# A four-layer hybrid decoder on one core: the layer-1 gate stored as twice its silu, the final gain moved to the last multiply, 1/rms per 512 tokens, and an earlier first norm

## The chip, the cores and the metric

The kernel runs on one core of a Trainium2 chip. The metric is the device time of one execution in microseconds; each comparison takes the median of several executions. TensorE (PE) does the matmuls, VectorE (DVE), ScalarE (ACT) and GpSimd (POOL) the elementwise work, and SyncE (SP), ACT and POOL issue DMAs. Each engine takes its instructions in the order in which they stand in its stream: one that waits holds back all behind it.

## The reference

The batch is 1, with 2048 tokens of width 1024 in fp32. The "layers" of the code are 0 and 1 (DEPTH = 2):

```
for i in range(2):
    hn = rmsnorm(h, norm_gain[i])
    if i == 0:   h = h + even_mixer(hn)      # retention and stick-breaking attention, gated
    else:        h = h + rwkv7_mixer(hn)     # r, k, v, g projections and a recurrence over tokens
    gate = sigmoid(h @ ple_gate[i])
    h = h + gate * (p[i] @ ple_proj[i])
return rmsnorm(h, final_gain)

# the part of rwkv7_mixer that the change touches
    y = head_norm(y, LNX_EPS) * lnx_g + lnx_b
    y = y + bonus
    out = (y * silu(g)) @ w_out
```

## The kernel before

**Tiling.** A token half `w` is 1024 tokens, a block `TB` is 512 tokens, a feature block is 128 rows (`NB` = 8 of them). The fp32 product is made of three matmul passes over a high and a low part of both operands (L239, L240, L241); `split` (L199 and L200) makes the parts: ACT casts the high part, and DVE or POOL subtracts it to get the low part. Raw weights pass through the buffer `wraw`, of which there is one; the split weights `w` are also written to DRAM as `parts` and read from there when they are used again.

**Order of the work.** Retention of half 0 (0 to 300 us), stick-breaking attention (to 500), `tail` of layer 0 (to 715: output projection, per-layer input, sum of squares `ssacc`), `l1_proj(0)` (to 1175: norm, the r, k, v, g projections and what the recurrence needs); retention and attention of half 1 (to 1690); `recur(0)`, the recurrence of half 0, merged with `tail_lean` for layer 0 of half 1 (to 2381, the first matmuls of `l1_proj(1)` beside its end); `l1_proj(1)` (to 2855); `recur(1)` merged with `tail_lean` for layer 1, three blocks of 512 tokens (to 3555); `tail` of layer 1 for the last block with `finish`, the final norm (to 3710). A scheduler that simulates the engines decides the order of the instructions on each engine when the program is built, so that a changed operation can reorder what stands around it.

**Places that the change touches.**

- At the start, `retention` loads x transposed for both blocks (`l0_in`, L352), then x by rows (`xt`, L367). ACT squares the rows and sums them (L369), DVE makes 1/rms (L335 to L342, L372), PE spreads it over the partitions (`rbp`, L375). The constants `k` (L144) and the `rope` table (L421) are loaded through SP.
- `l1_proj` adds `ssacc` up over the partitions by eight small matmuls (`ssp`, L991), makes 1/rms for 1024 tokens in one chain of DVE operations (L335 to L342), spreads it (`rbp`, L1046) and scales the activations into `hn` (L1064). In between, DVE splits weights for the other matmuls of that stage.
- `g_proj`, the last projection of `l1_proj`, copies each 128x512 result from PSUM to `ev` on ACT (L1108) and ACT issues its store.
- `post` in `recur` finishes a chunk of 64 tokens: POOL scales `y` and makes `vt` times the bonus `bon` (L1603), POOL multiplies `y` by the gain `lnx` (L1604), DVE adds the bias (L1605) and then adds `vt` to `y` (L1607). `gram` in `recur` is PE's L1396 with its evacuations on DVE (L1417, L1421) and ACT (L1420).
- `gated` in `tail_lean` makes m g sigmoid(g): DVE L866, ACT L867, DVE L868. `tail` uses silu on ACT (L713) and DVE L714.
- The final gain is applied in `tail_lean` by DVE (L949) and in `tail` by ACT (L779); `finish` and `tail` then multiply by the spread 1/rms (L830, L797).

## Time and profile before

| | before |
|---|---|
| median of 3 runs | 3716.74 us (3715.48 to 3717.23) |
| profiled execution | 3711.4 us |
| its span | 3709.6 us |
| granted clock, mean | 0.939 |
| PE busy | 3383.3 us, 91% |
| DVE busy | 1991.4 us, 54% |
| ACT busy | 1375.3 us, 37% |
| POOL busy | 971.0 us, 26% |
| DMA, mean | 181 GB/s |

The span is what the profile shows of the execution's own time. Busy shares are averages over stages with different limits; the rows further down are taken from single stages. In the timelines a bracket behind a row gives how long its engine sat idle before it, and what ended that.

### The profile page before, as it was taken

Reading aid. Unit: us, or ns where it says so; the run is one execution under the profiler, and the core shown is the slowest. Engines: PE = TensorE matmul, PEld = TensorE weight load, DVE = VectorE, ACT = ScalarE, POOL = GpSimd, SP = SyncE. Lnnn points to the kernel's source line nnn. Section 1 sums busy time; section 2 is a strip of 40 time slices with the busy share of each in tenths; the row PEclk is TensorE's granted clock in tenths of the full one; section 3 lists DMA queues with packets and bytes.
Section 4 is the critical chain, followed back from the end, with each engine's and each line's share of the span. In section 5 each row is a group of like instructions: output and inputs, shape, how many; then the busy total and the mean of one; then the engine's idle time right before and its main releaser. Section 6 shows DMA issues by size and latency. Waiting matters only on the chain.

```text
span 3709.6 us, 65403 instructions
## 1 busy us (share of the span) xinstructions
PE 3383.3 (91%) x25640; PEld 2694.0 (73%) x25640; DVE 1991.4 (54%) x3959; ACT 1375.3 (37%) x2671; POOL 971.0 (26%) x1019
## 2 busy tenths in 40 slices
PE   7999999899999999999879998699988698978968
PEld 6888878787666788888767776587656577767756
DVE  3435552452665333567856666641574477566543
ACT  4333442354564222445523333343453143223222
POOL 3345554300000222556512222200000243222322
PEclk9999999899999999999989998699999788979979
DMA  7259765655688216537367655333676777656485
GB/s 263 96 171 271 218 195 177 216 164 182 201 266 288 99 67 194 175 101 148 68 203 210 194 177 144 104 121 138 200 249 178 186 222 211 186 144 183 158 281 197
DMA packets 570788, 671.94 MB, mean 181 GB/s; under 512 B 215408, under 2 KB 416368, under 8 KB 539504
## 3 DMA queue, kind: packets, MB, share of 16 engines
q1 hardware_dynamic: 495072, 578.41, 50.2%
q0 software_dynamic: 40576, 33.56, 4.4%
q10 hardware_dynamic: 34832, 55.78, 4.1%
q8 instruction: 203, 3.33, 0.4%
q14 instruction: 105, 0.86, 0.1%
HBM read 419.50 MB, written 248.12 MB: 180 GB/s over the span
## 4 chain that ended last, share of the span: by engine, by line
PE 71%; DMA 10%; DVE 9%; ACT 3%; SPq 3%; issue 3%; POOL 1%; DVEq 0%; ACTq 0%; POOLq 0%
PE pj L239 17%; PE pj L240 17%; PE pj L241 17%; PE g L1396 2%; PE tp L654 1%; DMA nb<-nad 1%; DVE wb L1450 1%; DVE prd L1444 1%; PE lora L1266 1%; SPq L1429 1%; PE u L1516 1%; PE x L1538 1%; DMA xr<-ar 1%; PE z L625 1%; PE ot L240 1%
## 5 line engine op out<-in xcount | busy, mean ns | idle before, releaser
L239 PE MATMUL pj<-act,w 128*128 128x512 f32 x1216 | 498.5, 414 | 27.0 <-ACT act L199 10.5
L241 PE MATMUL pj<-act,w 128*128 128x512 f32 x1216 | 497.9, 410 | 6.0 <-POOL w L200 5.9
L240 PE MATMUL pj<-act,w 128*128 128x512 f32 x1216 | 496.9, 409 | 2.5 <-DVE act L200 1.7
L239 PE MATMUL pj<-xs,w 128*128 128x512 f32 x768 | 296.8, 401 | 21.0 <-ACT xs L199 9.5
L240 PE MATMUL pj<-xs,w 128*128 128x512 f32 x768 | 305.7, 399 | 6.3 <-DVE xs L200 6.2
L241 PE MATMUL pj<-xs,w 128*128 128x512 f32 x768 | 301.5, 395 | 0.0
L239 PEld LDWEIGHTS pj<-act,w 128*128 128x128 f32 x1216 | 238.3, 197 | 83.7 <-ACT act L199 13.1
L241 PEld LDWEIGHTS pj<-act,w 128*128 128x128 f32 x1216 | 238.4, 196 | 60.4 <-POOL w L200 9.0
L240 PEld LDWEIGHTS pj<-act,w 128*128 128x128 f32 x1216 | 238.9, 196 | 54.3 <-DVE act L200 3.0
L239 PE MATMUL pj<-w,act 128*128 128x512 f32 x640 | 257.7, 407 | 19.3 <-ACT w L199 9.8
L240 PE MATMUL pj<-w,act 128*128 128x512 f32 x640 | 256.7, 401 | 2.9 <-POOL w L200 2.9
L241 PE MATMUL pj<-w,act 128*128 128x512 f32 x640 | 254.3, 401 | 0.0
L636 DVE TENSOR_TENSOR_SCAN rr<-om,rr,ones 128x512 f32<-128x512 f32 (+3 forms) x160 | 202.0, 1274 | 46.8 <-ACT om L630 39.2
L645 POOL TENSOR_TENSOR be<-be,rr 128x512 f32<-128x512 f32 (+3 forms) x160 | 176.7, 1107 | 164.4 <-DVE rr L636 82.3
L200 POOL TENSOR_TENSOR w<-wraw,w 128x1024 fp32r<-128x1024 f32 x72 | 162.1, 2253 | 204.1 <-ACT w L199 198.1
L239 PEld LDWEIGHTS pj<-xs,w 128*128 128x128 f32 x768 | 145.4, 190 | 70.3 <-issue 14.5
L240 PEld LDWEIGHTS pj<-xs,w 128*128 128x128 f32 x768 | 145.9, 190 | 43.9 <-DVE xs L200 13.0
L241 PEld LDWEIGHTS pj<-xs,w 128*128 128x128 f32 x768 | 145.9, 190 | 33.9 <-issue 2.7
L1396 PE MATMUL g<-xr,kb 64*128 64x128 f32 x1024 | 116.8, 311 | 52.0 <-DVE grb L1421 23.0
L199 ACT CAST w<-wraw 128x1024 fp32r<-128x1024 f32 x105 | 104.6, 1000 | 144.7 <-DMA wraw<-in_even_w_in 38.7
L239 PEld LDWEIGHTS pj<-w,act 128*128 128x128 f32 x640 | 122.3, 192 | 48.4 <-ACT sg L448 12.1
L458 POOL TENSOR_SCALAR tst<-gs 128x128 f32<-128x128 f32 x64 | 34.4, 538 | 468.8 <-DMA gs<-gstate 246.5
(330 smaller groups left out, 7511.5 us busy)
## 6 DMA issues: line engine op xcount, KB each, us to landing
w<-parts SPq DMA_DIRECT2D x145, 1024.0 KB, 6.0
parts<-w SPq DMA_DIRECT2D x97, 1024.0 KB, 5.5
wraw<-in_odd_w_in SPq DMA_DIRECT2D x32, 512.0 KB, 7.2
ar<-ar SPq DMA_DIRECT2D x32, 512.0 KB, 4.4
w<-v SPq DMA_DIRECT2D x128, 128.0 KB, 3.8
xr<-ar SPq DMA_DIRECT2D x64, 256.0 KB, 5.5
kb<-kb SPq DMA_DIRECT2D x32, 512.0 KB, 5.1
kg<-dk POOLq DMA_DIRECT2D x24, 512.0 KB, 5.0
```

The costliest lines, as they stand in the source:

```text
L199: nc.scalar.copy(hi, src)
L200: (lo_eng or nc.vector).tensor_tensor(lo, src, hi.bitcast(F32), op=ALU.subtract)
L239: nc.tensor.matmul(ps, a[0], b[0], start=first, stop=False)
L240: nc.tensor.matmul(ps, a[0], b[1], start=False, stop=False)
L241: nc.tensor.matmul(ps, a[1], b[0], start=False, stop=last)
L625: nc.tensor.matmul(z[:, :kw], q[:, 1, qc], kt[:, 0, :kw], start=False, stop=True)
L636: nc.vector.tensor_tensor_scan(rr[:, 0:kw][:, ::-1], om[:, ::-1], self.ones.to_broadcast([P, kw]), rr[:, kw : kw + 1], op0=ALU.mult, op1=A ...
L645: nc.gpsimd.tensor_tensor(be, be, rr[:, 1 : kw + 1], op=ALU.mult)
L654: nc.tensor.transpose(tp[:, j], wt[qi][:, j * P : (j + 1) * P], self.ident)
L1266: nc.tensor.matmul(pss[j], w2[jw][hs, oc], mid[jm][hs, sl], start=n == 0, stop=n == 2)
L1396: nc.tensor.matmul(ps[:, j], kb[br, ob], xr[br, par, ob], start=True, stop=True)
L1429: nc.sync.dma_start(nad[b].rearrange("u r t -> r u t"), na[b * 16 : (b + 1) * 16, :, o : o + 16])
```

## The change

- Gates: ACT takes tanh(g/2) from PSUM and DVE computes (tanh + 1) g, which is 2 silu(g); that is stored. The bias of the head norm, halved, stands in the tile `hlb` and is added where the gate is applied: one DVE operation (m + hlb) g takes the place of L866, L867 and L868, and of L713 and L714 in layer 1. So that the sum stays right, `lnx` and `bon` are halved once per recurrence by two new ACT operations, the bias addition L1605 and its loads go.
- Final gain: L949 and L779 go; the last multiply becomes one DVE operation with the gain and the spread 1/rms.
- First norm: loads and squares of block 0 stand ahead of x of block 1; `k` goes to POOL's queue and `rope` to ACT's; for the first head of half 0 the low part of the weights is made by DVE instead of POOL.
- `l1_proj`: 1/rms is made for 512 tokens at a time by `rms(t)`, called at the first feature block of each token block.

```diff
-        nc.sync.dma_start(k, ins["c_mat"][:, 0:C_SCAN])
+        nc.gpsimd.dma_start(k, ins["c_mat"][:, 0:C_SCAN])
...
+                        self.lo_eng = nc.vector if w == 0 else nc.gpsimd
...
-                nc.sync.dma_start(rope, self.i["c_rope"][w * HT : (w + 1) * HT, :].rearrange("(t p) c -> p t c", p=P))
-                self.l0_in(w, sx, 1, range(0, NB))
-                self.l0_stats(w, sx, pq)
+                nc.scalar.dma_start(rope, self.i["c_rope"][w * HT : (w + 1) * HT, :].rearrange("(t p) c -> p t c", p=P))
+                self.lo_eng = nc.gpsimd
                 for tb in range(NTB):
+                    if tb:
+                        self.l0_in(w, sx, tb, range(0, NB))
+                    self.l0_stats(w, sx, pq, [tb])
...
-                        nc.scalar.activation(g, g, AF.Silu)
-                        nc.vector.tensor_tensor(m, m, g, op=ALU.mult)
+                        if l == 0:
+                            nc.scalar.activation(g, g, AF.Silu)
+                            nc.vector.tensor_tensor(m, m, g, op=ALU.mult)
+                        else:
+                            nc.vector.scalar_tensor_tensor(
+                                m, m, self.hlb[:, d : d + 1], g, op0=ALU.add, op1=ALU.mult
+                            )
...
-                    o = sb.tile([P, TB], F32, tag="o", name=self.u("o"))
+                    o = h1[ob] if l else sb.tile([P, TB], F32, tag="o", name=self.u("o"))
...
-                    else:
-                        nc.scalar.activation(h1[ob], o, AF.Copy, scale=self.col(V_GF, ob))
...
-                    nc.vector.tensor_tensor(o, rbp, h1[ob][:, tok(t)], op=ALU.mult)
+                    nc.vector.scalar_tensor_tensor(
+                        o, h1[ob][:, tok(t)], self.col(V_GF, ob), rbp, op0=ALU.mult, op1=ALU.mult
+                    )
...
-                nc.vector.tensor_tensor(m, m, g, op=ALU.mult)
-                nc.scalar.activation(g, g, AF.Sigmoid)
-                nc.vector.tensor_tensor(m, m, g, op=ALU.mult)
+                if l == 0:
+                    nc.vector.tensor_tensor(m, m, g, op=ALU.mult)
+                    nc.scalar.activation(g, g, AF.Sigmoid)
+                    nc.vector.tensor_tensor(m, m, g, op=ALU.mult)
+                else:
+                    nc.vector.scalar_tensor_tensor(m, m, self.hlb[:, d : d + 1], g, op0=ALU.add, op1=ALU.mult)
...
-                if l == 1:
-                    nc.vector.tensor_scalar_mul(o, o, self.col(V_GF, ob))
...
-            rs = self.token_rstd(ev, psn, "rnp")
-            rb = [ev.tile([P, TB], F32, tag="L" if t else "sg", name=self.u("rb")) for t in range(NTB)]
-            for t in range(NTB):
-                rbp = pj[0].tile([P, TB], F32, tag="proj", name=self.u("rbp"))
+            rb, hn = [], []
+
+            def rms(t):
+                rs = self.token_rstd(ev, psn, "rnp", range(4 * t, 4 * t + 4))
+                rb.append(ev.tile([P, TB], F32, tag="L" if t else "sg", name=self.u("rb")))
+                rbp = psn.tile([P, TB], F32, tag="rnp", name=self.u("rbp"))
...
             def normed(d, t):
+                if d == 0:
+                    rms(t)
...
+            def twice_silu(dst):
+                def evac(t, ps):
+                    e = ev.tile([P, TB], F32, tag="ev", name=self.u("ev"), bufs=2)
+                    nc.scalar.activation(e, ps, AF.Tanh, scale=0.5)
+                    nc.vector.scalar_tensor_tensor(e, e, 1.0, ps, op0=ALU.add, op1=ALU.mult)
+                    nc.scalar.dma_start(dst[:, t * TB : (t + 1) * TB], e)
+
+                return evac
+
             def g_proj():
-                yield from self.proj_pairs(load(3), mix(3), lambda ob: to_dram(d_g[ob]), pj)
+                yield from self.proj_pairs(load(3), mix(3), lambda ob: twice_silu(d_g[ob]), pj)
...
-            nc.gpsimd.tensor_tensor(y, y, lnx[0][0], op=ALU.mult)
-            nc.vector.tensor_tensor(vt, vt, lnx[1][0], op=ALU.add)
+            nc.gpsimd.tensor_tensor(y, y, lnx, op=ALU.mult)
...
             for par in range(2):
-                for t, src in lnx:
-                    nc.sync.dma_start(t[half(par)], src[par].unsqueeze(0).to_broadcast([C, NB, C]))
+                nc.sync.dma_start(lnx[half(par)], gain[par].unsqueeze(0).to_broadcast([C, NB, C]))
                 nc.sync.dma_start(bonus[half(par)], self.d_b[par].rearrange("(c t) o -> t c o", t=C))
+            nc.scalar.activation(lnx, lnx, AF.Copy, scale=0.5)
+            nc.scalar.activation(bonus, bonus, AF.Copy, scale=0.5)
```

Three places of the streams follow. The first is SP's, from its first `xt` load to its fourth, at the start of the program (`x` is x transposed, 256 KB; `wraw` a pair of 256 KB weight loads; `parts` a 1 MB store of split weights; `xt` 512 KB). Before:

```order
L367 DMA xt_230<-in_x 128x1024
L352 DMA x_212<-in_xT 128x512
L367 DMA xt_234<-in_x 128x1024
L221 DMA parts_161<-w_155 128x2048
L214 DMA wraw_188<-in_even_w_in 128x4x128 x2
L352 DMA x_216<-in_xT 128x512
L352 DMA x_220<-in_xT 128x512
L352 DMA x_224<-in_xT 128x512
L367 DMA xt_238<-in_x 128x1024
L221 DMA parts_177<-w_171 128x2048
L214 DMA wraw_685<-in_even_w_in 128x4x128 x2
L367 DMA xt_242<-in_x 128x1024
```

In the changed kernel the same place, from the second `parts` store on (all 16 loads of x transposed stand ahead of the fourth `xt` in both):

```order
L223 DMA parts_163<-w_157 128x2048
L216 DMA wraw_190<-in_even_w_in 128x4x128 x2
L354 DMA x_258<-in_xT 128x512
L354 DMA x_262<-in_xT 128x512
L354 DMA x_266<-in_xT 128x512
L354 DMA x_270<-in_xT 128x512
L370 DMA xt_208<-in_x 128x1024
L370 DMA xt_212<-in_x 128x1024
L223 DMA parts_179<-w_173 128x2048
L216 DMA wraw_688<-in_even_w_in 128x4x128 x2
```

The fourth `xt` now stands ahead of the third `parts` store and of the fifth pair of `wraw` loads; before, both stood ahead of it.

The second place is DVE's stream at the start of `l1_proj(0)`, from the last addition to `ssacc` (token block 1) to the last step of the first 1/rms. Before, with 1/rms for 1024 tokens:

```order
L775 TENSOR_TENSOR ssacc<-ssacc,g_6256 128x512
...
L1063 COPY hn_6455<-hnlast 128x1
L335 TENSOR_SCALAR rs_1238_6350<-ssp_6341 128x8
L336 TENSOR_SCALAR rs_1240_6352<-ssp_6341 128x8
L200 TENSOR_TENSOR w_6595<-wraw_6596,w_6595 128x1024
...
L200 TENSOR_TENSOR w_6635<-wraw_6636,w_6635 128x1024
...
L342 SCALAR_TENSOR_TENSOR rs_1239_6351<-rs_1238_6350,rs_1239_6351 128x8
L1064 SCALAR_TENSOR_TENSOR hn_6381<-hx_6382,vec,rb_6366 128x512
```

In the changed kernel, with 1/rms for the first 512 tokens:

```order
L786 TENSOR_TENSOR ssacc<-ssacc,g_6259 128x512
...
L1077 COPY hn_6447<-hnlast 128x1
L337 TENSOR_SCALAR rs_1240_6350<-ssp_6345 128x4
L338 TENSOR_SCALAR rs_1242_6352<-ssp_6345 128x4
L339 TENSOR_SCALAR rs_1241_6351<-rs_1240_6350 128x4
L202 TENSOR_TENSOR w_6615<-wraw_6616,w_6615 128x1024
...
L202 TENSOR_TENSOR w_6655<-wraw_6656,w_6655 128x1024
...
L1078 SCALAR_TENSOR_TENSOR hn_6373<-hx_6374,vec,rb_6366 128x512
```

The first 1/rms still stands behind the last addition to `ssacc` and has the same two weight splits within it.

The third place is DVE's stream at the start of `recur(1)`, between two evacuations of `gram` (`xr` and `grb` are what `gram` writes from PSUM). Before:

```order
L1417 TENSOR_TENSOR xr_26647<-g_26753,k 64x512
L1417 TENSOR_TENSOR xr_26647<-g_26754,k 64x512
L1421 TENSOR_TENSOR grb_26752<-g_26753,k 64x256
L1421 TENSOR_TENSOR grb_26752<-g_26754,k 64x256
L1605 TENSOR_TENSOR vt_27819<-vt_27819,lnx_26510 128x512
L1417 TENSOR_TENSOR xr_26647<-g_26802,k 64x512
L1417 TENSOR_TENSOR xr_26647<-g_26803,k 64x512
```

In the changed kernel:

```order
L1438 TENSOR_TENSOR xr_26683<-g_26789,k 64x512
L1438 TENSOR_TENSOR xr_26683<-g_26790,k 64x512
L1442 TENSOR_TENSOR grb_26788<-g_26789,k 64x256
L1442 TENSOR_TENSOR grb_26788<-g_26790,k 64x256
L1438 TENSOR_TENSOR xr_26683<-g_26838,k 64x512
L1438 TENSOR_TENSOR xr_26683<-g_26839,k 64x512
```

The bias addition, which waits for POOL, no longer stands between two pairs of `gram`. On ACT, though, the two new operations stand at this place, ahead of the same `gram`'s evacuations:

```order
L1441 ACTIVATE na_26694<-g_26736 64x4x64
L1669 ACTIVATE lnx_26562<-lnx_26562 128x512
L1670 ACTIVATE bon_26563<-bon_26563 128x128
L1561 COPY xs_27534<-x_27517 128x512
L1441 ACTIVATE na_26694<-g_26789 64x4x64
L1441 ACTIVATE na_26694<-g_26790 64x4x64
L201 CAST w_26714<-wraw_26715 128x1024
```

Both wait for the loads of `lnx` and `bon` that SP issues at this place, and the weight cast stands behind them.

## Rows read from the trace of the kernel before

**Rows 1.** The page, parts 1 and 4: busy time of the engines; the chain that ended last.

```profile
PE 3383.3 (91%) x25640; PEld 2694.0 (73%) x25640; DVE 1991.4 (54%) x3959; ACT 1375.3 (37%) x2671; POOL 971.0 (26%) x1019
...
PE 71%; DMA 10%; DVE 9%; ACT 3%; SPq 3%; issue 3%; POOL 1%; DVEq 0%; ACTq 0%; POOLq 0%
```

**Rows 2.** Stretches of the span: busy time (x instructions), granted clock, DMA share.

```profile
core 0: us, PE busy (x) PEld busy (x) DVE busy (x) ACT busy (x) POOL busy (x), PEclk, DMA share, GB/s
...
1075.00:1175.00 100.00, 100.00 (x421) 71.19 (x419) 62.38 (x110) 56.75 (x100) 0.00 (x0) 1.00 0.78 263
...
2281.00:2381.00 100.00, 63.86 (x1284) 54.86 (x1284) 58.79 (x176) 24.67 (x50) 21.36 (x18) 0.64 0.35 96
...
2868.00:2910.00 42.00, 22.13 (x131) 17.02 (x128) 17.66 (x42) 7.27 (x15) 7.19 (x5) 0.72 0.84 205
2910.00:3555.00 645.00, 576.81 (x7454) 457.49 (x7453) 405.35 (x931) 193.34 (x383) 192.50 (x140) 0.88 0.62 184
3550.00:3600.00 50.00, 23.68 (x86) 18.01 (x84) 26.09 (x59) 10.39 (x16) 7.32 (x6) 0.63 0.94 325
```

**Rows 3.** Waits of PE, 0 to 75 us: total us, times, longest.

```profile
PE rbp L375 <- DVE rs L342: 5.7, 1, 5.7
```

**Rows 4.** The DMA view, 5 to 45 us.

```profile
DMA packets 10815, 15.26 MB, mean 382 GB/s; under 512 B 592, under 2 KB 7701, under 8 KB 10258
...
parts<-w SPq DMA_DIRECT2D x5, 1024.0 KB, 9.3
```

**Rows 5.** Timeline of ACT, 34 to 46 us: start, duration, operation, idle before.

```profile
39.46 1.06 ACT L369 ACTIVATE sq<-xt 128x1024 bf16<-128x1024 f32 x1 [0.24 <-DMA xt<-in_x]
```

**Rows 6.** Timeline of DVE, 39 to 45 us.

```profile
40.64 1.02 DVE L335 TENSOR_SCALAR rs<-st 128x4 f32<-128x4 f32 x1 [5.44 <-ACT sq L369]
...
44.09 0.19 DVE L426 TENSOR_TENSOR qks<-rs,k 128x32 f32<-128x32 f32 x1
```

**Rows 7.** Waits of PE, 700 to 740 us.

```profile
PE rbp L1046 <- DVE rs L342: 5.9, 1, 5.9
PE ssp L991 <- DVE ssacc L775: 4.2, 1, 4.2
```

**Rows 8.** Timeline of DVE, 715 to 725.5 us.

```profile
722.18 1.23 DVE L200 TENSOR_TENSOR w<-wraw,w 128x1024 fp32r<-128x1024 f32 x1 [0.95 <-ACT w L199]
```

**Rows 9.** Timeline of DVE, 1864 to 1890 us.

```profile
1866.97 0.69 DVE L1605 TENSOR_TENSOR vt<-vt,lnx 128x512 f32<-128x512 f32 x1 [2.40 <-POOL vt L1603]
```

**Rows 10.** Line L1605, whole span: idle time of DVE before it (us, times).

```profile
  POOL vt L1603: 57.1, 18
```

**Rows 11.** Timeline of all engines, 2880 to 2894 us.

```profile
2882.63 0.39 SPq L214 DMA_DIRECT2D wraw<-in_odd_w_out  x1
...
2888.61 0.69 DVE L1605 TENSOR_TENSOR vt<-vt,lnx 128x512 f32<-128x512 f32 x1 [14.81 <-POOL vt L1603]
...
2891.12 2.61 PE L1396 MATMUL g<-xr,kb 64*128 64x128 f32 x16 [15.30 <-DVE grb L1421]
2892.23 1.04 ACT L199 CAST w<-wraw 128x1024 fp32r<-128x1024 f32 x1 [1.07 <-DMA wraw<-in_odd_w_out]
```

**Rows 12.** Waits of PE, 2910 to 3555 us.

```profile
PE t L1506 <- DVE f L1499: 7.1, 3, 3.0
...
PE f L1495 <- DVE t L1489: 0.4, 1, 0.4
```

**Rows 13.** Groups of instructions by line and shape: count, busy us, mean ns, idle before.

```profile
L1108 ACT COPY ev<-pj 128x512 f32<-128x512 f32 x96 | 55.8, 586 | 166.7 <-PE pj L241 137.1 <-DMA r<-ev 12.6 <-DMA kk<-ev 9.9
...
L552 DVE TENSOR_TENSOR pf<-pj,rb 128x512 f32<-128x512 f32 x48 | 32.7, 682 | 21.1 <-PE pj L241 14.1 <-DMA dg<-pf 5.8 <-DMA parts<-w 0.2
...
L866 DVE TENSOR_TENSOR stage<-stage,g 128x512 f32<-128x512 f32 x26 | 24.0, 923 | 28.5 <-DMA g<-g 17.5 <-DMA g<-dg 6.3 <-DMA stage<-yT 4.8
...
L949 DVE TENSOR_SCALAR o<-o,vec 128x512 f32<-128x512 f32 x24 | 22.4, 931 | 6.3 <-ACT g L946 4.7 <-ACT ssacc L944 1.4
```

**Rows 14.** Waits of PE, 3550 to 3709 us.

```profile
PE pj L239 <- ACT act L199: 10.5, 6, 8.8
```

More of the change, by code (lines that the diff above doesn't have):

```diff
@@ L73 @@
 C_N = C_HX + 4 * P
-V_G0, V_G1, V_GF, V_MU, V_W0, V_A0, V_KK, V_KA, V_RK, V_GN = 0, 1, 2, 3, 9, 10, 11, 12, 13, 14
-V_N = 15
+V_G0, V_G1, V_GF, V_MU, V_W0, V_A0, V_KK, V_KA, V_RK, V_GN, V_LB = 0, 1, 2, 3, 9, 10, 11, 12, 13, 14, 15
+V_N = 16
 def constants():
@@ L191, in load_vectors @@
         nc.vector.tensor_scalar_mul(self.hka, ka, 0.5)
+        self.hlb = self.cst.tile([P, NB], F32, name="hlb")
+        nc.vector.tensor_scalar_mul(self.hlb, v[:, V_LB * NB : (V_LB + 1) * NB], 0.5)
     def col(self, which, b):
@@ L356, in l0_in, with l0_stats @@
             nc.vector.scalar_tensor_tensor(lo, x, g, hi.bitcast(F32), op0=ALU.mult, op1=ALU.subtract)
-    def l0_stats(self, w, sb, psp):
+    def l0_stats(self, w, sb, psp, tbs):
         nc = self.nc
-        self.rb0 = self.dr.tile([P, HT], F32, name=self.u("rb0"))
-        st = sb.tile([P, NTT], F32, name=self.u("st"), tag="st", bufs=1)
-        for tb in range(NTB):
+        if 0 in tbs:
+            self.rb0 = self.dr.tile([P, HT], F32, name=self.u("rb0"))
+        st = sb.tile([P, NTT], F32, name=self.u("st"), tag="st", bufs=2)
+        for tb in tbs:
             for t in range(4 * tb, 4 * tb + 4):
@@ L829, in finish @@
             o = sb.tile([P, TB], F32, tag="o", name=self.u("fo"))
-            nc.vector.tensor_tensor(o, rbp, xs.pop(0), op=ALU.mult)
+            nc.vector.scalar_tensor_tensor(o, xs.pop(0), self.col(V_GF, ob), rbp, op0=ALU.mult, op1=ALU.mult)
             nc.sync.dma_start(self.out_at(w, ob, t), o)
@@ L1038, in head_sums @@
                 nc.tensor.matmul(ps[rows(ob, t)], hsum[:, ob // 2], x, start=ob < 2, stop=ob >= NB - 2)
-            rs = self.token_rstd(ev, psn, "rnp")
-            rb = [ev.tile([P, TB], F32, tag="L" if t else "sg", name=self.u("rb")) for t in range(NTB)]
-            for t in range(NTB):
-                rbp = pj[0].tile([P, TB], F32, tag="proj", name=self.u("rbp"))
+            rb, hn = [], []
[3 more added lines that the diff above has]
+                rbp = psn.tile([P, TB], F32, tag="rnp", name=self.u("rbp"))
                 for j in range(4):
-                    jj = t * 4 + j
                     nc.tensor.matmul(
                         rbp[:, j * P : (j + 1) * P],
-                        rs[:, jj : jj + 1].to_broadcast([P, P]),
+                        rs[:, j : j + 1].to_broadcast([P, P]),
                         self.ident,
@@ L1053, in l1_proj @@
                 nc.scalar.copy(rb[t], rbp)
-            hn = []
             def normed(d, t):
+                if d == 0:
+                    rms(t)
                 if t == 0:
@@ L1357, in recur @@
         TF = lambda tag, shape, bufs: fin.tile(shape, F32, tag=tag, name=self.u(tag), bufs=bufs)
-        lnx = []
-        for nm in ("rwkv_lnx_gain", "rwkv_lnx_bias"):
-            t = fin.tile([P, NB, C], F32, name=self.u("lnx"), bufs=1)
-            lnx.append((t, i[nm][0].rearrange("(o s c) -> s o c", s=2, c=C)))
+        lnx = fin.tile([P, NB, C], F32, name=self.u("lnx"), bufs=1)
         bonus = fin.tile([P, NCH, NB], F32, name=self.u("bon"), bufs=1)
@@ L1644, in main @@
                 yield PRE[2]
+            gain = i["rwkv_lnx_gain"][0].rearrange("(o s c) -> s o c", s=2, c=C)
             for par in range(2):
-                for t, src in lnx:
-                    nc.sync.dma_start(t[half(par)], src[par].unsqueeze(0).to_broadcast([C, NB, C]))
+                nc.sync.dma_start(lnx[half(par)], gain[par].unsqueeze(0).to_broadcast([C, NB, C]))
                 nc.sync.dma_start(bonus[half(par)], self.d_b[par].rearrange("(c t) o -> t c o", t=C))
+            nc.scalar.activation(lnx, lnx, AF.Copy, scale=0.5)
+            nc.scalar.activation(bonus, bonus, AF.Copy, scale=0.5)
             b = None
@@ L1792 @@
     "x", "ple_proj", "ple_gate", "even_w_in", "even_w_out", "odd_w_in", "odd_w_out", "rwkv_w1", "rwkv_w2",
-    "rwkv_a1", "rwkv_a2", "rwkv_lnx_gain", "rwkv_lnx_bias",
+    "rwkv_a1", "rwkv_a2", "rwkv_lnx_gain",
 ]
@@ L1809, in vectors @@
         (V_RK, a("rwkv_r_k", 0)),
+        (V_LB, a("rwkv_lnx_bias", 0)),
     ):
```

## The prediction

> **What bounds the kernel now.** I read the page first [rows 1]: TensorE is busy for 3383 of 3709.6 us, so only some 326 us are to be had without taking matmuls away, and the change takes none of the large ones away. The chain that ended last runs through PE for 71%, through DMA for 10% and DVE for 9%. DVE is busy for 54%: its work as such bounds nothing, but where PE stands still it often waits for DVE. So I cut the span into stretches [rows 2] and asked each stretch that the change touches what PE waits for. Most of the 326 us lie in four places: the start, the change from the layer-0 tail to `l1_proj` (around 720 and 2330 us), the first 35 us of `recur(1)`, and the two recurrences with their many waits of 1 to 4 us. The middle of the projections has nothing to give: PE works for 100.00 of 100 us from 1075 to 1175 [rows 2], the end of `l1_proj(0)` with `g_proj`.
>
> **The change part by part.** All terms are in us against the profiled execution (3711.4, of it 3709.6 span); it lies 5.3 below the median of the runs, which I add at the end.
>
> *A, the start.* PE waits 5.7 us for 1/rms [rows 3]. The chain: the fourth row block lands and ACT squares it from 39.46 [rows 5], DVE's fifteen small operations run from 40.64 to 44.09 [rows 6], then PE goes on. The chain itself stays as long, so what counts is when the fourth block lands. Loads and stores run at 382 GB/s from 5 to 45 us [rows 4], so landing times follow the bytes ahead. SP's order moves a 1 MB `parts` store [rows 4] and a pair of 256 KB weight loads behind the fourth block: 1.5 MB, at 382 GB/s 4 us. PE has its last matmuls of block 0 a little before the wait, and the weight split there goes from POOL to DVE, which only helps. I take -4; bounds -5.7 (the whole wait) and +1 (`k` and `rope` now start together with the first x loads).
>
> A rule bears on the two moved queues. The Trainium skill, "Trainium Kernel Development and Optimization", section "Key Constraints", says that DMAs issued from SP, ACT and POOL all run on the same 16 engines and that issuing from several saves issue time only. By it, moving `k` and `rope` (1 MB together) gains no bytes, and A stays at -4; were the other queues extra bandwidth, 1 MB less ahead would be 2.7 us more, and A would reach its bound of -5.7. No row here separates the two.
>
> *B, the norm of `l1_proj`.* At 712 to 730 us PE waits 4.2 us for the last `ssacc` and 5.9 us for 1/rms [rows 7]. Making 1/rms for 512 tokens could start before the second block's sum is ready. But DVE's order shows the first chain still behind that sum, the eight `hnlast` copies and with both weight splits inside. The second split starts at 722.18 after waiting 0.95 for ACT's cast of the weights [rows 8]: that sets its end, and one small step fewer follows it. So -0.3 at the first call. The second call adds thirteen small operations of about 0.2 us (the spacing in [rows 6]) = 2.6 us of DVE, and at `l1_proj(1)` the same form holds. Bounds: -5.9 (the wait goes) and +2.6 (the second chain is exposed).
>
> *C, `g_proj`.* 32 evacuations, so far one ACT copy of 0.586 [rows 13], become tanh plus a DVE operation reading PSUM; the nearest row for that is 0.682 for L552 [rows 13], together 1.3 us. Is it covered? A pair of output blocks ends with nine matmuls after its first result is complete; at 100 us for 421 matmuls [rows 2] these last 2.1 us. So the first buffer comes free 0.8 us before it is wanted, unless DVE is late by more. DVE is busy for 62% there [rows 2], mostly with single operations of 0.7 us. I take +1 over the eight pairs of both halves; bounds 0 and +24 (DVE 3 us late at each pair).
>
> The Trainium skill's "Perfetto Trace Analysis", section "Optimizing Scalar/DVE Operations", gives DVE 125 ns of access overhead on PSUM and ACT 51 ns. By it each of these DVE operations would be 0.07 us dearer than one of ACT, an estimate of 2.4 us if all 32 were exposed; the rows' 0.682 against 0.586 makes it 3.1.
>
> *D, the first recurrence.* L1605 waits for POOL 57.1 us in 18 places [rows 10] and holds back all that stands behind it on DVE. Around 1867 it waited 2.40 us and then took 0.69 [rows 9], ahead of work that PE needs for its next step. I take -2 for both such places of this stretch; bounds -6 (POOL wait and operation twice) and 0.
>
> *E, the start of `recur(1)`.* Here stands PE's longest stall of that stretch, 15.3 us on an evacuation of `gram` which stands behind L1605, and L1605 waited 14.81 us for POOL [rows 11]. L1605 goes. It would be easy to book 15 us. But look at what is late next. The weight load of the tail was issued at 2882.63 and ACT, free by then, waited 1.07 us for it and cast it at 2892.23 [rows 11]; PE's stretch after 2891 is work with weights that were already there, then it needs these. Pulled forward, PE does that work early and waits for the weights. These move only by the two bias loads (some tenths of a us of SP's time each, as the 0.39 of the load in [rows 11]) that SP no longer issues ahead of them. Also two new ACT operations wait at this place for `lnx` and `bon`. I take -2; bounds -15.3 and +4 (ACT held by these loads, with the weight cast behind).
>
> *F, the body of `recur(1)`.* From 2910 to 3555 PE idles 68 us [rows 2], 23.1 of them in seven groups of waits for DVE, from 7.1 down to 0.4 [rows 12]. DVE loses 16 gate operations of 0.92 (L866), 24 gain operations of 0.93 (L949) [rows 13] and 15 of L1605 at 0.69 [rows 9]: 47 us of its 405 [rows 2], 12%. If its waits shrink in proportion, -2.8; ACT loses 16 operations too. I take -3; bounds -12 (half of these waits) and +5 (the scheduler's new order is worse in a stretch of some 7450 matmuls).
>
> *G, the end.* PE waits 10.5 us for ACT's casts of the gated rows [rows 14]. The silu, about as long as the copy in [rows 13], leaves that chain, but the stage is fed by DMA (share 0.94, [rows 2]), so most of it stays. The last eight multiplies become 0.07 us longer each, +0.5. I take -1.5; bounds -4 and +0.5.
>
> **Sum.** -4 -0.3 +1 -2 -2 -3 -1.5 = -11.8: 3699.6 for an execution like the profiled one, 3705 beside the median. The end of the first recurrence (2281 to 2381, PE 63.86 of 100 us, [rows 2]) is reordered too; I find no sign in it and take 0, within 6 either way.
>
> **The rivals.** About 0.2% (7.4 us) is what a measurement of this kernel can tell from no change: below 3709.3 is faster, above 3724.2 slower.
>
> *The stalls only move (same).* E gives back 15 us to weights and DMA, D's waits pass to the next POOL result, A's gain is eaten as x of block 1 lands later. For it: DMA is at 0.84 in the stretch of E and 0.94 in that of G [rows 2]. Against it: A's wait is one chain with nothing else late beside it. Only F and G hold half: 3711.4 - 2.3 + 5.3 = 3714.
>
> *The whole stall is had (much faster).* If the weights of E land earlier because `gram` no longer holds the loads that SP queues between, -13 more, and the body gives 8 more than F: 3684. For it: 57.1 us of L1605 waits [rows 10] is the largest single item that the change removes. Against it: the cast at 2892.23.
>
> *`g_proj` holds its buffers (slower).* Each result stays in PSUM until DVE has read it, and ACT's store waits for DVE in ACT's own queue, ahead of the next tanh and cast. It decides from about 2.5 us late at each of the eight pairs: 8 x 2.5 = 20, less the 12.8 of the other terms; at 3 us late 3711.4 - 12.8 + 24 + 5.3 = 3728. For it: PE has no idle time there to hide in. Against it: the cover of 0.8 us and DVE's short operations.
>
> **How the numbers follow.** Forecast (the small gains, 3698 to 3711) 0.45, nearly all of it faster; the whole stall 0.13; stalls only move 0.25; `g_proj` late 0.10, and a worse order in the recurrences (F and the end of the first recurrence at their bad bounds, 3711.4 - 8.8 + 5 + 6 + 5.3 = 3719, more if both merged stretches suffer) 0.07. That makes faster 0.57, same 0.26, slower 0.17. The range runs from 3686, near the full stall, to 3727, near the late `g_proj`; the forecast's own is 3698 to 3711.
>
> **What would show it.** A: PE's wait for `rbp` starts the retention about 4 us earlier (40 instead of 43.9). B: the `rbp` wait near 725 us is still there. C: no PE waits on DVE between 1075 and 1175. E: the 15.3 us wait is gone, but the first cast of new weights comes at about 2891 less what was gained before, and PE waits for weights just ahead of it. F: fewer waits on DVE. I am wrong if that cast moves up by over 5 us, if PE waits on `ev` or on DVE in `g_proj`, or if the recurrences' idle time changes by over 12 us either way.

## The result, and the profile after

The changed kernel takes 3687.22 us (median of 4 runs, 3679.78 to 3697.76), the kernel before 3716.79 (4 runs): ratio 0.9917, 95% interval 0.9898 to 0.9936. That is 29.6 us faster, where 11.8 were forecast. Three executions of other groups (one of before, one each of e12 and e16 below) took 9.3 to 15.0 ms and are left out of all medians, ranges and ratios. The profiled execution lies 7.4 us below its median, the one of before 5.3 below, so the two profiles differ by 31.6 us.

The page of the changed kernel, parts 1 and 4, answers to [rows 1]:

```profile
span 3678.0 us, 65350 instructions
...
PE 3372.8 (92%) x25640; PEld 2687.7 (73%) x25640; DVE 1951.1 (53%) x3942; ACT 1347.6 (37%) x2629; POOL 958.2 (26%) x1016
...
PE 70%; DMA 11%; DVE 10%; ACT 3%; SPq 2%; issue 2%; POOL 1%; ACTq 0%; DVEq 0%; POOLq 0%
```

The same 25640 matmuls keep PE busy for 10.5 us less: a third of the gain is not idle time but matmuls that ran faster. Two marks cut each trace into the same pieces: a recurrence begins with its first L1396 matmul; the first ends with its last L1538, the second is taken with all that follows it. The stretch view of before, both pieces (us, PE busy (x), granted clock, DMA share, GB/s):

```profile
1701.60:2362.70 661.10, 566.69 (x7658) 0.90 0.58 158
2863.40:3709.60 846.20, 716.99 (x8104) 0.86 0.65 196
```

The changed kernel:

```profile
1701.30:2352.60 651.30, 567.60 (x7631) 0.90 0.59 160
2856.10:3678.00 821.90, 709.25 (x8107) 0.89 0.67 200
```

All of the gain is in these two pieces: -9.8 and -24.3 us; what lies before the first is -0.3, what lies between them +2.9. In the second piece PE idles 112.7 us instead of 129.2, and is busy 7.7 us less at a granted clock of 0.89 instead of 0.86. The clock has two levels, 2.4 GHz and 1.2 GHz, so a mean of 0.86 is 28% of 846 us at the lower one, some 237 us, and 0.89 is 22% of 822 us, some 181 us (the means are read to two digits, so each may be off by 8 us).

How that comes about shows at the start of `recur(1)`. Stretches of before, same columns:

```profile
2875.00:2891.00 16.00, 0.82 (x6) 0.50 1.04 247
2891.00:2898.00 7.00, 6.84 (x26) 0.51 0.60 173
2898.00:2906.00 8.00, 6.82 (x40) 1.00 0.63 180
```

PE stood still for most of 16 us; then it worked 6.84 of 7 us, still at the lower level, and did 26 matmuls; at the higher level it did 40 in 6.82 us. Sixteen small ones of `gram` are in both counts, so it is 10 large ones against 24. An idle stretch is paid twice.

### The profile page after: what moved, and what is told of

Read it like the earlier page. It is cut to its first block, busy times and chain, and to the rows that moved or that the text cites. A ratio compares the mean times of both kernels' runs of the same rounds, so it can differ in the third digit from the quotient of the medians.

```text
span 3678.0 us, 65350 instructions
## 1 busy us (share of the span) xinstructions
PE 3372.8 (92%) x25640; PEld 2687.7 (73%) x25640; DVE 1951.1 (53%) x3942; ACT 1347.6 (37%) x2629; POOL 958.2 (26%) x1016
## 4 chain that ended last, share of the span: by engine, by line
PE 70%; DMA 11%; DVE 10%; ACT 3%; SPq 2%; issue 2%; POOL 1%; ACTq 0%; DVEq 0%; POOLq 0%
PE pj L241 17%; PE pj L242 17%; PE pj L243 17%; PE g L1417 2%; DMA xr<-ar 1%; PE tp L660 1%; DMA w<-parts 1%; PE x L1559 1%; DVE prd L1465 1%; DVE wb L1471 1%; PE u L1537 1%; PE lora L1289 1%; DVE rr L642 1%; PE ot L242 1%; DMA g<-g 1%
## 5 line engine op out<-in xcount | busy, mean ns | idle before, releaser
L202 POOL TENSOR_TENSOR w<-wraw,w 128x1024 fp32r<-128x1024 f32 x68 | 150.2, 2211 | 455.8 <-ACT w L201 401.8
L241 PEld LDWEIGHTS pj<-w,act 128*128 128x128 f32 x640 | 122.7, 192 | 56.8 <-ACT sg L454 16.8
L202 DVE TENSOR_TENSOR wT<-tp,wT 128x512 fp32r<-128x512 f32 (+3 forms) x160 | 94.7, 600 | 92.6 <-ACT wT L201 91.7
```

The lines of the kernel that those rows point to most:

```text
L202: (lo_eng or nc.vector).tensor_tensor(lo, src, hi.bitcast(F32), op=ALU.subtract)
L241: nc.tensor.matmul(ps, a[0], b[0], start=first, stop=False)
```

## The experiments

The parts are taken from the change as it stands; "doubled copy" is one 0.6 us ACT operation of `l1_proj` issued twice, which does nothing. The pieces are from each kernel's profiled execution, one each, so a difference of a few us between two pieces says nothing: before and e3 have the same order of matmuls in the first recurrence, and 7 us between them. Within a group of runs on one chip the kernel before had medians from 3717.0 to 3721.7 us, with single runs from 3707.6 to 3732.5.

| kernel | L1605 | gate operations | median us | first recurrence | second and end |
|---|---|---|---|---|---|
| before | yes | 3 | 3716.8 | 661 | 846 |
| e1 first norm alone | yes | 3 | 3740.0 | 679 | 860 |
| e3 final gain alone | yes | 3 | 3713.1 | 669 | 842 |
| e4 1/rms alone | yes | 3 | 3702.6 | 663 | 823 |
| e5 doubled copy alone | yes | 3 | 3739.4 | 667 | 849 |
| e8 changed, without gate part | yes | 3 | 3726.7 | 684 | 842 |
| e11 L1605 on other data | altered | 3 | 3708.1 | 663 | 842 |
| e12 L1605 on POOL | altered | 3 | 3723.0 | 671 | 845 |
| e10 2 silu, L1605 kept | yes | 1 | 3700.0 | 667 | 824 |
| e16 e10 with doubled copy | yes | 1 | 3715.3 | 675 | 836 |
| e9 L1605 and bias left out | no | 3 | 3719.8 | 674 | 841 |
| e18 e9 with doubled copy | no | 3 | 3693.6 | 647 | 841 |
| e13 changed, raw gates | no | 3 | 3691.5 | 657 | 826 |
| changed | no | 1 | 3687.2 | 651 | 822 |
| e2 gate part alone | no | 1 | 3681.8 | 653 | 814 |
| e6 changed, doubled copy | no | 1 | 3687.1 | 654 | 819 |
| e7 changed, without first norm | no | 1 | 3694.6 | 657 | 817 |
| e14 gate and 1/rms parts | no | 1 | 3703.1 | 658 | 825 |
| e15 e9 and e10 together | no | 1 | 3684.9 | 653 | 829 |
| e17 changed, final gain as before | no | 1 | 3672.6 | 648 | 820 |

**The four parts, each alone (e1 to e4).** The edit of each is its hunks of the diff ahead of the prediction; one line of each:

```diff
+                    self.l0_stats(w, sx, pq, [tb])                                  # e1, with k, rope, lo_eng
+                    nc.vector.scalar_tensor_tensor(m, m, self.hlb[:, d : d + 1], g, op0=ALU.add, op1=ALU.mult)   # e2, with twice_silu, lnx, bonus
-                    nc.vector.tensor_scalar_mul(o, o, self.col(V_GF, ob))           # e3, with L779, L797, L830
+                    rms(t)                                                          # e4
```

> The kernel before with the first-norm part alone (k and rope on other queues, block 0's squares first, DVE splits the first weights). Theory 1 (each part acts in its own stage): the first rbp comes 4 us earlier, some 2 us of that is left when the second rbp is done, and the whole is 0 to 4 us faster; the recurrences keep their times within 2 us. Theory 2 (the scheduler's new order does it, whatever the edit): the recurrences move by 5 us or more although nothing in them was edited.

> The kernel before with the gate part alone (2 silu stored, bias in hlb, L1605 and the bias loads gone, two ACT halvings). Theory 1: this part holds most of the gain, 14 to 20 us: the start of the second recurrence about 7 us shorter, its body about 10 shorter. Theory 2 (the DVE time of the final gain, L949, weighs as much as that of the gate): 5 to 10 us only. Theory of the prediction: about 6 us (terms C to F without L949).

> The kernel before with the merged final gain alone (L949 and L779 gone, the last multiplies with two factors). Theory 1 (DVE work off the path is worth little): 0 to 4 us faster. Theory 2 (DVE time in the second recurrence is worth what it takes): 24 x 0.93 us = 22 us less DVE work, of which a third or more comes back: 7 us or more.

> The kernel before with 1/rms for 512 tokens at a time alone. Theory 1 (the prediction): the wait for rbp at 725 us stays, the whole within 3 us of before. Theory 2: at the start of the second l1_proj, where it lies beside the first recurrence's end, the smaller first step lets the recurrence's end go 8 us earlier (2282 to 2363 us took 8 us less in the changed kernel), so that this part gives 6 to 10 us.

Ratios to before: e1 1.0062 (1.0043 to 1.0081), e2 0.9903 (0.9874 to 0.9932), e3 0.9991 (0.9976 to 1.0006), e4 0.9959 (0.9944 to 0.9974). The first-norm part alone costs 23 us. Its own place did what was expected (first `rbp` at 39.5 us instead of 43.9); the loss is in the recurrences, 18 and 14 us longer, which it does not touch. e4's gain of 14 us is in the second piece too (823 us), not in `l1_proj` nor at the end of the first recurrence. Of what was on record only Theory 2 of e1, the scheduler's new order, allows this. e2 gains 35 us, more than any of its three theories gave it.

**An edit that does nothing (e5), and the same on the changed kernel (e6).**

```diff
             nc.scalar.copy(hexp, hx0)
+            nc.scalar.copy(hexp, hx0)
```

> The kernel before with one 0.6 us ACT copy in each l1_proj issued twice (the same values written again): nothing of the change. It makes the scheduler order the matmuls of both recurrences anew. Theory 2 (the order that the scheduler happens to find in the two merged stretches is worth 10 to 25 us by itself): the time moves by over 7 us, either way, and the difference lies between 1700 and 2370 us or between 2860 and 3550 us. Theory 1 (each edit acts in its own place): within 3 us of before, at most 1.2 us slower for the copies.

> The changed kernel with the same doubled copy. Its first recurrence keeps the changed kernel's order of matmuls, its second gets another. Theory 2: the time of the first recurrence stays within 4 us of that of the changed kernel, that of the second moves by over 5 us. Theory 1: the whole within 3 us of the changed kernel.

e5: 1.0056 (1.0038 to 1.0074), 22 us slower for an operation of 0.6 us per `l1_proj`. Its pieces:

```profile
1704.10:2371.10 667.00, 575.73 (x7630) 0.89 0.58 156
2877.00:3726.40 849.40, 709.88 (x8104) 0.87 0.65 195
```

Its PE stream agrees with that of before until the first `l1_proj`; in the recurrences hundreds of rows stand elsewhere. Theory 2 was right on the size and only half right on the place: this profiled execution is 16.8 us longer than that of before, 9.1 of it in the two pieces and 7.7 ahead of and between them. e6 took 0.9912 (0.9883 to 0.9942), 3687.1 us against 3687.2. What was expected of its order was mistaken: there the doubled copy changed no row of PE's stream in either recurrence. So e6 is the control: the same order, the same time, with the copy in it.

**Pieces taken back (e7, e8).** The changed kernel without the hunks of e1 (e7) and without those of e2 (e8):

```diff
-                    self.l0_stats(w, sx, pq, [tb])                                  # e7, with k, rope, lo_eng
-                yield from self.proj_pairs(load(3), mix(3), lambda ob: twice_silu(d_g[ob]), pj)   # e8, with hlb, lnx, bonus
```

> The changed kernel without the first-norm part. If the parts simply add (the first-norm part alone cost 23 us): 3664 us, 23 faster than the changed kernel, a version that beats both. Theory 2: the 23 us were an order found for that kernel alone; here the first rbp comes 4 us later and the rest is another draw, 3675 to 3700 us.

> The changed kernel without the gate part (first norm, final gain and 1/rms parts alone). If the parts add (+23 -4 -14): 3722 us, 5 slower than before. If the gate part has an effect of its own whatever the order (no L1605 that waits for POOL, 30 us less DVE work in the second recurrence): at least 15 us slower than the changed kernel, 3702 us or more, in the second recurrence. Theory 2: anything from 3690 to 3735.

e7: 0.9927 (0.9901 to 0.9953), 7 us slower than the changed kernel, not 23 faster: the loss of e1 does not carry over. e8: 1.0019 (0.9999 to 1.0038), 40 us slower than the changed kernel, and by the pieces 33 us of it in the first recurrence, where no gate of layer 1 is applied. In both of these pairs (before and e2, e8 and changed) the gate part is worth 35 to 40 us; a third pair, below, gives nothing.

**L1605 alone, in three forms (e9, e11, e12), and the gates alone (e10).** All four start from the kernel before.

```diff
-            nc.vector.tensor_tensor(vt, vt, lnx[1][0], op=ALU.add)              # e9, with its loads
+                    nc.vector.scalar_tensor_tensor(m, m, 0.5, g, op0=ALU.mult, op1=ALU.mult)   # e10, with twice_silu
...
-            nc.vector.tensor_tensor(vt, vt, lnx[1][0], op=ALU.add)
+            nc.vector.tensor_tensor(lnx[1][0], lnx[1][0], bc(rs), op=ALU.max)   # e11
+            nc.gpsimd.tensor_tensor(vt, vt, lnx[1][0], op=ALU.add)              # e12
```

> The kernel before without the bias of the head norm at all (L1605 and its four loads gone; the output lacks the bias), gates as before. So far kernels with L1605 took 661 to 684 us for the first recurrence and 632 to 662 for the second, those with the gate part 651 to 657 and 615 to 629. Theory A (L1605, which makes DVE wait for POOL, is the effect): the first recurrence takes 650 to 658, the second 620 to 635, the whole 15 to 30 us faster than before. Theory B (the gates' three operations are it): the first recurrence 661 or more, the whole within 12 us of before.

> The kernel before with 2 silu stored and one DVE operation per gate (halved there), L1605 and the bias loads kept. Theory A: the first recurrence, where no gate of layer 1 is applied, 661 to 684 as in all kernels with L1605; the second 10 us shorter at most; the whole 3705 to 3735. Theory B: the second recurrence 615 to 630, the whole under 3700.

> The kernel before, with L1605 not on vt but on the bias tile itself and DVE's own rs (the same 128x512 elements on DVE, the same loads, no wait for POOL; the bias doesn't reach the output). Theory A1 (the wait for POOL is what costs): as without L1605, the first recurrence 650 to 658 us, the whole 15 to 30 us faster. Theory A2 (DVE's time for it, 32 x 0.7 us, or the bias loads cost): the first recurrence 661 or more, the whole within 12 us of before.

> The kernel before with L1605 on POOL instead of DVE: the bias stays, DVE neither waits nor works for it, POOL takes some 1.1 us more per chunk. Theory A (either form): the first recurrence 650 to 660 us, the whole 10 to 30 us faster than before. Theory 2 alone (only the order that the scheduler finds counts): any first recurrence from 650 to 685.

e9: 1.0001 (0.9987 to 1.0015); e11 0.9970 (0.9957 to 0.9983); e12 1.0008 (0.9994 to 1.0021); e10 0.9948 (0.9930 to 0.9966). Theory A fell, by these single kernels: the first recurrence took 674 us in e9, 663 in e11 and 671 in e12. Theory B held in e9 but not in e10, whose second recurrence took 641 us to its last L1538 (615 to 630 were expected) and 824 with its end.

**More draws of the same edits (e13 to e16, e18).** e14 is e2 with e4, e15 e9 with e10, e16 and e18 are e10 and e9 with the doubled copy; e13 is the changed kernel with `g` stored raw, `hlb` not halved and no halving of `lnx` and `bonus`:

```diff
                     nc.vector.scalar_tensor_tensor(m, m, self.hlb[:, d : d + 1], g, op0=ALU.add, op1=ALU.mult)
+                    nc.scalar.activation(g, g, AF.Sigmoid)
+                    nc.vector.tensor_tensor(m, m, g, op=ALU.mult)
```

> The changed kernel with the gate stored raw again: the bias still comes in at the gate ((m + bias) g on DVE, sigmoid on ACT, a second multiply on DVE; silu on ACT in the last tail), no halving of gain and bonus. All else as in the changed kernel, the output is the reference's. Theory C (one operation per gate, with no trip to ACT and back, is what shortens the second recurrence and the end: 814 to 824 us with it, 840 to 860 without it in all but one kernel): the second recurrence and the end take 835 us or more, the whole 10 to 25 us slower than the changed kernel. Theory 2 (only the order): 814 to 860, anything.

> The kernel before with the gate part and the 1/rms part. Its first recurrence has an order of matmuls unlike that of any kernel so far. Theory C: second recurrence and end 810 to 825 us. For the first recurrence: if the gate part's edits shorten it, 650 to 658 us in this order too; if the order did (the four kernels at 651 to 657 have two orders only), anything from 650 to 685. If parts add, the whole is 3668 us and beats the changed kernel.

> The kernel before with one DVE operation per gate (2 silu stored, halved there) and without the bias of the head norm (L1605 and its loads gone, the output lacks the bias): the gate part without the two ACT halvings and the bias. Theory C: second recurrence and end 810 to 825 us, the whole 3680 to 3700. Theory 2: anything.

> The kernel with 2 silu stored and L1605 kept, with the doubled 0.6 us copy in each l1_proj, so another order in both recurrences. Theory C: second recurrence and end again 815 to 828 us (824 without the copy), the whole within 12 us of 3700. Theory 2: anything from 814 to 860.

> The kernel before without the bias of the head norm (L1605 and its loads gone, three operations per gate, the output lacks the bias), with the doubled 0.6 us copy: another order in both recurrences. In eight kernels without L1605 the first recurrence took 651 to 658 us in seven and 674 in the one of these two edits alone. Theory D (without L1605 the first recurrence is some 14 us shorter on the average over orders, the 674 was an order): 650 to 662 us, the whole 3690 to 3712. Theory 2 (L1605 does nothing, the seven were orders): 662 or more.

Ratios: e13 0.9930 (0.9911 to 0.9948), e14 0.9956 (0.9940 to 0.9972), e15 0.9916 (0.9893 to 0.9938), e16 0.9993 (0.9979 to 1.0008), e18 0.9931 (0.9906 to 0.9955). e13 missed what Theory C asked (826, not 835 or more), and so did e15 (829) and e16 (836). e18 against e9, the same edit in another order, is 26 us: no single kernel settles anything here. Nor does e14: it is e4 with the gate part, and takes 3703.1 us against 3702.6, so that in this pair the gate part gave nothing. The first recurrence took 658 us in e14, not in an order of its own as expected but with the matmuls in the order of e7 (657); in e18 it took 647.

**An order chosen (e17).** The changed kernel with L779, L949, L797 and L830 as before: more DVE work, and in each recurrence the PE order of a kernel that was fast there.

```diff
+                if l == 1:
+                    nc.vector.tensor_scalar_mul(o, o, self.col(V_GF, ob))
```

> The changed kernel with the final gain as before (the 24 DVE gain operations and the 8 on ACT are back, 22 us of DVE work in the second recurrence). Its matmuls stand in the order of the changed kernel in the first recurrence (two rows apart) and exactly in that of the gate part alone in the second. Theory 2 (the order of PE decides, the final gain's DVE work hardly counts): first recurrence 651 to 655 us as in the changed kernel, second recurrence and end 812 to 820 as with the gate part alone, the whole 3670 to 3682, a version that beats both. If the DVE work of the final gain counts, 3690 or more.

e17: 0.9868 (0.9849 to 0.9888), 3672.6 us, 14.6 faster than the changed kernel, which it beats by leaving a part of the change out. Its pieces:

```profile
1701.00:2349.40 648.40, 569.42 (x7630) 0.90 0.58 161
2848.60:3668.30 819.70, 702.34 (x8107) 0.89 0.68 202
```

The forecast from the orders alone (651 to 655, and 812 to 820) held within 3 us, although DVE is busy for 461.5 us in the second piece, against 446.6 in the changed kernel.

**What the draws say together.** The kernels of the table fall into four cells; left out are the altered L1605, and e6 and e17, whose orders of matmuls repeat those of others in both recurrences (before and e3, e7 and e14 share one in the first alone). Means of the medians: L1605 and three operations 3723.1 (six kernels, 3702.6 to 3740.0); L1605 and one operation 3707.7 (two); no L1605 and three 3701.6 (three); neither, one operation 3690.3 (five, 3681.8 to 3703.1). So one operation instead of three is worth 15 us with L1605 and 11 without, and L1605 21 and 17: together 33 us, with an uncertainty of about 7 (the outer cells' standard deviations of 15 and 9 us over the roots of six and five, added in squares), as far as the orders are independent draws. An additive fit to the sixteen gives L1605 20 us and the gates 13, each with an uncertainty of about 7, so the gates' half alone is not clear of nothing. Around such a mean an order adds or takes 10 to 20 us: the 29.6 us of the change agree with the gate part's mean effect, but how much of them is the order of this one kernel can't be told.

The pieces, all twenty kernels, separate the two better. In the first recurrence the ten kernels with L1605 in some form take 670 us in the mean (661 to 684), the ten without 655 (647 to 674). In the second recurrence and the end, where the gates of layer 1 are applied, the eleven kernels with three operations take 842 (823 to 860), the nine with one 823 (814 to 836); seven of those nine also lack L1605 while only three of the eleven do, so part of these 19 us is L1605's.

What of L1605 it is stays open. In e11 it doesn't wait for POOL and in e12 it isn't on DVE, and their first recurrences (663 and 671) are still among those with it; both keep the bias loads. Two draws are too few, and an edit with the loads alone was not tried.

## Why the prediction was wrong, point by point

The sign was right, and the sum was less than half. That the time lies inside the wide range is luck: it is 11 us below the forecast's own range (3698 to 3711), and the low end of 3686 stood for a rival that did not happen as described. All three signs of being wrong came: the cast moved up by 17.0 us (9.8 beyond what was gained ahead of it), PE waited on `ev` in `g_proj`, and PE's idle time fell by 10.7 us in the first piece and 16.6 in the second. The step that failed is the sizing of D, E and F by the waits that were seen. The waits of PE for DVE in the one order of before (F: "If its waits shrink in proportion, -2.8") were taken as all that there was to gain; they did not shrink, 23.1 us before and 23.4 after, while their stretch got 12.2 us shorter. The lower clock after idle stretches was left out: in the second piece PE is busy 7.7 us less for the same work. And the scheduler's new order was allowed 5 and 6 us, where a doubled copy alone moved the whole by 22. By which step the gate part makes the recurrences shorter stays open.

*A, forecast -4.* Right at its place, lost behind it. Waits of PE in the changed kernel, 0 to 75 us, to set beside [rows 3]:

```profile
PE pj L241 <- ACT w L201: 13.5, 2, 12.0
PE pj L241 <- ACT sg L454: 3.7, 1, 3.7
PE rbp L378 <- DVE rs L344: 1.6, 1, 1.6
```

The first `rbp` comes at 39.67 us, 4.2 earlier: the fourth square starts 3.4 us earlier (36.08 instead of 39.46), and DVE's chain, forecast to stay as long, is 0.9 shorter. The two moved queues gave nothing beyond that; loads and stores ran at 381 GB/s from 5 to 45 us, against 382 before. This agrees with the Trainium skill, "Trainium Kernel Development and Optimization", section "Key Constraints", though no run moves the queues alone. PE then waits 3.7 us for ACT instead of 1.3, the second `rbp` is 2.1 us earlier, and at the first matmul of the recurrence 0.3 us is left. Against e7, the changed kernel without this part, more is left: there the first recurrence begins at 1712.6 us, 11.3 later.

*B, forecast -0.3.* Right, as no gain. Waits of PE, 700 to 740 us, to set beside [rows 7]:

```profile
PE rbp L1059 <- DVE rs L344: 11.8, 1, 11.8
```

The two waits of 4.2 and 5.9 us have become one of 11.8: a wait that vanishes from a list has often only joined the next.

*C, forecast +1.* Right inside the first `g_proj`, undersized behind it. From 1073 to 1173 us PE waits for nothing; in the second `g_proj`, 2735 to 2846 us, there is one wait on the new operation, in the waits of PE; the operation itself is in the groups by line and shape:

```profile
PE pj L241 <- DVE ev L1250: 5.3, 1, 5.3
```

```profile
L1250 DVE SCALAR_TENSOR_TENSOR ev<-ev,pj 128x512 f32<-128x512 f32 x32 | 21.7, 684 | 26.7 <-ACT ev L1249 26.7
```

At 0.684 us it costs what L552 did, 0.682 [rows 13]. The slower rival did not happen: PE was not kept waiting at eight pairs but at one. But the price of the first `g_proj` comes just behind it, where PE waits longer for ACT as the next stage begins. Timeline of PE, before and changed:

```profile
1208.34 0.80 PE L239 MATMUL pj<-w,act 128*128 128x512 f32 x1 [3.45 <-ACT sg L448]
```

```profile
1209.67 0.79 PE L241 MATMUL pj<-w,act 128*128 128x512 f32 x1 [5.79 <-ACT sg L454]
```

From PE's 5000th to its 5400th matmul (1133.1 to 1234.5 us before) the changed kernel takes 4.3 us more; the nine kernels with 2 silu stored take 2.9 to 4.3 us more than before, the ten others from 0.3 less to 1.4 more. The stretch between the recurrences, with the second `g_proj`, is 2.9 us longer.

*D, forecast -2.* Undersized. The first recurrence got 9.8 us shorter in the profile and is 15 us shorter in the mean over the kernels without L1605. D counted two of the seven waits of L1605 in that recurrence. Waits of DVE of before, 1701.6 to 2362.7 us:

```profile
DVE vt L1605 <- POOL vt L1603: 17.3, 7, 3.5
```

Counting all seven would not have explained it: in e11 L1605 waits for nothing, and its first recurrence took 663 us.

*E, forecast -2.* The mechanism held, the size did not. Timeline of the changed kernel, 2866 to 2881 us:

```profile
2866.20 0.43 SPq L216 DMA_DIRECT2D wraw<-in_odd_w_out  x1
...
2871.10 1.04 POOL L1624 TENSOR_TENSOR vt<-vt,bon 128x512 f32<-128x512 f32 x1 [27.91 <-DMA vt<-v]
...
2875.20 1.04 ACT L201 CAST w<-wraw 128x1024 fp32r<-128x1024 f32 x1 [8.90 <-DMA wraw<-in_odd_w_out]
...
2876.30 0.79 PE L241 MATMUL pj<-act,w 128*128 128x512 f32 x1 [8.33 <-ACT w L201]
```

As forecast, the 15.3 us wait on `gram` [rows 11] is gone, and the weights are what PE waits for now, 8.3 us. But the cast moved by 17.0 us, and by 9.8 counted from the recurrence's first matmul (-7.25 us), not by the 1.3 of two bias loads. SP's run of issues from `w` to `wraw`, without the bias loads, takes 26.8 us (2839.36 to 2866.20) instead of 31.3 (2851.34 to 2882.63), which is 4.5 of the 9.8; the run also begins 4.7 us earlier against that first matmul, and the weights come 0.6 us faster. Its first issue, before and changed:

```profile
2851.34 2.40 SPq L1383 DMA_DIRECT2D w<-v  x4
```

```profile
2839.36 2.40 SPq L1404 DMA_DIRECT2D w<-v  x4
```

The two ACT halvings cost nothing visible: ACT did not wait for their loads here.

*F, forecast -3.* Undersized by the most, and its mechanism did not show. The second recurrence to its last L1538 is 18.8 us shorter; 6.6 of it are E (the `gram` that ran at 2901.08 runs at 2887.25, 13.8 us earlier, of which 7.25 were there when the recurrence began); the rest, 12.2, is the body. Stretches of the body and of the end behind it, before and changed (us, PE busy (x), granted clock, DMA share, GB/s):

```profile
2910.00:3511.50 601.50, 536.34 (x7104) 0.87 0.63 183
3511.50:3709.60 198.10, 154.27 (x820) 0.87 0.67 234
```

```profile
2896.20:3485.40 589.20, 534.70 (x7130) 0.89 0.66 190
3485.40:3678.00 192.60, 146.95 (x790) 0.88 0.67 232
```

PE idles 10.7 us less in the body, but not on DVE. Its waits for DVE in the changed kernel, 2896.2 to 3485.3 us, add up to 23.4 us, against 23.1 [rows 12]:

```profile
PE x L1559 <- DVE w L1583: 8.3, 6, 4.5
PE kt L1547 <- DVE tds L1530: 6.9, 2, 4.9
PE g L1417 <- DVE grb L1442: 4.6, 2, 3.3
PE yt L1632 <- DVE y L1627: 1.8, 1, 1.8
PE t L1527 <- DVE f L1520: 1.1, 1, 1.1
PE f L1516 <- DVE t L1510: 0.7, 1, 0.7
```

What is gone are waits of before, 2910 to 3555 us, that the profile puts down to no engine ("issue"); the body of the changed kernel has none:

```profile
PE t L1481 <- issue: 4.6, 4, 1.3
...
PE x L1538 <- issue: 3.9, 1, 3.9
```

The final gain, on which F put 24 of its 55 operations, measured 4 us in e3 (not clear of no change), and e17 does without it. The gates and L1605, the other 31, carry the effect as far as the cells show one (13 and 20 us over the whole kernel), but not by fewer waits of PE for DVE.

*G, forecast -1.5.* Not shown. From the last L1538 to the end it is 192.6 us instead of 198.1, but 30 matmuls of the end now stand ahead of that mark, and PE's idle time there is 45.6 us instead of 43.8. The wait for ACT's casts, 10.5 us in [rows 14], is 14.1 in the changed kernel; the wait for `y` went from 11.1 to 4.5. Among other kernels with one operation per gate this end takes 183 us in e10 and 199 in e16.

*The rivals.* "The stalls only move" happened at A, B and half of E. "The whole stall is had" came nearest in time (3684), but not by its mechanism: the cast of the weights did limit E.

## What to carry to other kernels

Where a scheduler orders the instructions, the first thing to measure is an edit that does nothing: here it moved the time by 22 us, so a single comparison under that size says little of an edit, and an edit's worth is a mean over several orders. What waits for an instruction in one order is a poor price of it: e11 removed all 57.1 us of L1605's waits and gained about 11 us, and PE's waits for DVE stayed as long where F's stretch got shorter. The matmuls that run at the lower clock after a stall belong to its price. An order can also be kept on purpose: leaving a harmless part out (e17) gave more than adding it.

## What the runs showed of the hardware

In the kernel before the granted clock read 0.51 from 2891 to 2898 us, although PE was busy for 6.84 of these 7 us, and 1.00 from there to 2906; the matmuls of a stall's end pay for the stall. The same eight small matmuls show it at the start, in the timelines of before and of the changed kernel, after a wait of 5.7 us (granted clock 0.50) and one of 1.6 (1.00):

```profile
43.91 2.08 PE L375 MATMUL rbp<-k,rs 128*128 128x128 f32 x8 [5.71 <-DVE rs L342]
```

```profile
39.67 1.16 PE L378 MATMUL rbp<-k,rs 128*128 128x128 f32 x8 [1.65 <-DVE rs L344]
```

And one program varies more than its first runs told: before, 3715.5 to 3717.2 us in 4 runs, 3707.6 to 3732.5 in 22 others, with medians 0.2 us apart.
